# Four key groups moved into the first part's norms, six modulations on VectorE, token products of 512 columns

## Chip, cores and metric

One program runs on one core of a Trainium2 chip. The metric is the device time of one execution in microseconds; the runs before the change took 1834.9 to 1837.41 us, with a median of 1836.98.

## What is computed

Two transformer parts run one after the other on 256 tokens of width 1024, all in fp32. The reference, cut to what matters here:

```python
def first_block(x, c, ...):
    c_act = silu(c)                                    # one row of 1024
    for l in range(2):
        mod = c_act @ w_ada[l] + b_ada[l]              # six rows of 1024
        sh1, sc1, g1, sh2, sc2, g2 = split(mod, 6)
        h = rmsnorm(x, norm_mix_g[l]) * (1 + sc1) + sh1
        z = h @ w_in[l]
        o = concat([swa(z), mla(z), nsa(z), moba(z)])  # four attentions, 4 heads each
        x = x + g1 * (o @ w_out[l])
        h = rmsnorm(x, norm_mlp_g[l]) * (1 + sc2) + sh2
        x = x + g2 * (square(relu(h @ w_up[l])) @ w_down[l])
    return rmsnorm(x, final_norm_g)

def second_block(x, mem, ...):
    for l in range(2):
        z, xbc, dt, dq, dk, dv, dg, cq, cg, gl = split(x @ w_in[l])
        y_ssd, y_diff = ssd(z, xbc, dt), diff_attention(dq, dk, dv) * silu(dg)
        mk, mv = split(mem @ w_mem_kv[l])              # keys, values of 256 memory tokens
        y_cross = cross_attention(cq, mk, mv) * silu(cg)
        merged = sum of gates[i] * (branch i @ its weights)
        x = layernorm(ALPHA * x + merged @ w_out[l])
```

## The kernel before

**Weights.** Every weight passes once, as tiles `w` of 128 x 1024 fp32 (0.5 MB). The list `wq` holds them in the order in which they're used; `stream` appends to it. `next_w` takes the next one, and on the way loads the first 8 entries of the list (`AHEAD_W`, through SP's queue, into a ring of `NW` = 8 tiles) and splits the first 4: ScalarE rounds the tile to fp32r (`wh`, line 290), VectorE subtracts (`wl`, line 292). Products run as three fp32r matmuls, high by high, low by high and high by low. Tiles of the modulations (`w_ada`) and of the two compressions aren't split; they stay in their ring slot until they've been multiplied.

**Products.** `gemm` queues a product of 256 output columns as two pieces of 24 matmuls of 128x128 by 128x256, summed in one bank of PSUM. With `tok=True` tokens lie on the partitions: the activations are the loaded operand, 256 weight columns stream, and a bank holds both token halves. This form makes the memory's values, the difference attention's values `dv`, the last output, and two small products of the first part.

**The order of the work.** The queue `q` holds pieces under tags; `fill(n)` emits the next n, `need(tag)` all up to the last with that tag. The framework then orders each engine's instructions by priority (splits and norm chains stand higher) along a simulated timeline. What is left in `q` when a norm starts runs while the norm's chain (square, sum over partitions, power of -0.5, spread, scale, shift) goes through the other engines.

**Modulations.** Each of the twelve (layer, slot) pairs has four steps of two tiles. `ada_step` does them on TensorE (four blocks of 32 columns, fp32, two instructions each: 64 for a pair), `ada_pool` on GpSimd, as a product per partition and a sum, whose rows `ada_rows` adds up over the partitions with eight short matmuls; `ada_end` transposes the result into `mod`. GpSimd has (1,0), (1,1) and (1,5), during the feed-forward parts. TensorE has the other nine: (0,0) and (0,1) at the start, (0,2) to (0,4) in layer 0's attention, (0,5) in its second norm (tag `norm`), (1,2) and (1,3) between the layers (tag `next`), (1,4) in layer 1's second norm.

**The memory's keys and values.** `mem_gemm` makes them in eight groups of 256 columns, four of keys and four of values. Layer 0's six first groups run at the start, mixed with modulation steps, its last two in the first part's last norm, after the memory has been loaded again (`late_mem`). Layer 1's eight run at the end of layer 0 of the second part, whose layer norm asks for 2, 4 and 2 pieces between its steps and leaves the last eight to its scale and shift.

**Units.** Activations live in a ring of `NU` = 11 tiles of 128 x 2048 fp32. Three banks of PSUM (`gbank`) serve the products.

**The last output.** `finish` adds the residual and computes mean and variance by 256 columns, then normalizes.

## Time and profile before

| | |
|---|---|
| median of 3 runs | 1836.98 us |
| the profiled execution's own time | 1838.83 us |
| its span | 1837.0 us |
| mean granted clock of TensorE | 0.992 |
| instructions | 37186 |
| VectorE busy | 73% |
| ScalarE busy | 55% |
| GpSimd busy | 20% |
| read from HBM | 339.01 MB |

Times within the trace count from the span's start. Up to 61 us the start's products and modulations run, up to 205 layer 0's attention, up to 404 its feed-forward part; layer 1 goes from there to 746, and the second part from 770 to the end. Matmuls are pipelined, so a matmul's duration is longer than the step to the next. A wait for several semaphores is put down to the one that came last.

### The profile page before, as it was taken

To read this page: it belongs to the slowest core of one execution; us is meant where nothing else is said; L and a number is where in the kernel's file an instruction comes from. 1 tells how busy PE (TensorE), PEld (TensorE's weight loads), DVE (VectorE), ACT (ScalarE), POOL (GpSimd) and SP (SyncE) were. 2 spreads that over 40 slices of the span, in tenths; PEclk is the share of its full clock that TensorE was granted. 3 is DMA by queue.
4 is the path that set the end of the run, shared out by engine and by line. 5 is a ranking of instruction groups with operands and counts; after the bars stand their busy time and mean duration, and the time that the engine had idled before them with its cause. 6 is when DMAs were issued, how large, how long until landed. Compare 5 with 4: busy or idle time off the path is not lost.

```text
span 1837.0 us, 37186 instructions
## 1 busy us (share of the span) xinstructions
PE 1791.6 (98%) x14800; PEld 1696.7 (92%) x14800; DVE 1334.8 (73%) x2212; ACT 1017.1 (55%) x1882; POOL 358.9 (20%) x291
## 2 busy tenths in 40 slices
PE   7999999999998999999999999999999999999998
PEld 6878799987878999999999999999999999999998
DVE  4575775756778655798897897566687897997566
ACT  4354444444545444557777575454556687675552
POOL 0000271800007300002444202200001445202200
PEclk9999999999998999999999999999999999999999
DMA  9873886757447655554444644465553445554451
GB/s 335 317 246 129 301 272 197 258 197 294 130 138 282 230 182 183 168 171 140 143 162 154 191 161 148 166 205 175 193 175 130 148 160 162 181 166 168 153 183 60
DMA packets 98223, 346.88 MB, mean 189 GB/s; under 512 B 12288, under 2 KB 13440, under 8 KB 97792
## 3 DMA queue, kind: packets, MB, share of 16 engines
q1 hardware_dynamic: 98048, 344.50, 55.5%
q8 instruction: 116, 1.90, 0.4%
q14 instruction: 59, 0.48, 0.1%
HBM read 339.01 MB, written 1.05 MB: 185 GB/s over the span
## 4 chain that ended last, share of the span: by engine, by line
PE 90%; DVE 3%; ACT 2%; DMA 2%; issue 1%; POOL 0%; POOLq 0%; SPq 0%; DVEq 0%; ACTq 0%
PE g L318 68%; PE acc L318 10%; PE yps L318 2%; DVE wl L292 1%; PE sc L318 1%; PE ada L318 1%; PE ds L318 1%; PE o L318 1%; DMA w<-w_ada 1%; ACT wh L290 1%; PE do L318 1%; PE xs L318 1%; PE xo L318 1%; DMA w<-w_up 1%; PE tw L1153 1%
## 5 line engine op out<-in xcount | busy, mean ns | idle before, releaser
L292 DVE TENSOR_TENSOR wl<-w,wh 128x1024 fp32r<-128x1024 f32 x518 | 664.3, 1285 | 337.7 <-ACT wh L290 335.5
L290 ACT CAST wh<-w 128x1024 fp32r<-128x1024 f32 x518 | 540.6, 1047 | 510.9 <-PE g L318 328.3
L318 PE MATMUL g<-xh,wh 128*128 128x256 f32 x1664 | 477.1, 287 | 0.7 <-DVE cv L1234 0.4
L318 PE MATMUL g<-xl,wh 128*128 128x256 f32 x1664 | 472.3, 284 | 0.0
L318 PE MATMUL g<-xh,wl 128*128 128x256 f32 x1664 | 471.7, 284 | 0.0
L318 PEld LDWEIGHTS g<-xh,wh 128*128 128x128 f32 x1664 | 319.3, 192 | 13.0 <-issue 6.9
L318 PEld LDWEIGHTS g<-xl,wh 128*128 128x128 f32 x1664 | 319.4, 192 | 0.8 <-issue 0.7
L318 PEld LDWEIGHTS g<-xh,wl 128*128 128x128 f32 x1664 | 319.4, 192 | 0.1
L318 PE MATMUL g<-ah,wh 128*128 128x256 f32 x736 | 210.4, 288 | 4.2 <-ACT ah L552 4.2
L318 PE MATMUL g<-al,wh 128*128 128x256 f32 x736 | 210.6, 287 | 2.5 <-DVE al L553 2.5
L318 PE MATMUL g<-ah,wl 128*128 128x256 f32 x736 | 210.8, 287 | 0.7 <-DVE wl L292 0.7
L358 POOL TENSOR_TENSOR rsy<-rv,mhalf 128x2 f32<-128x2 f32 (+1 forms) x14 | 13.4, 958 | 938.8 <-DVE rv L375 831.1
L318 PE MATMUL acc<-pt,wh 128*128 128x256 f32 x1024 | 183.1, 280 | 0.0
L1452 POOL PARTITION_BROADCAST E<-rows x64 | 96.6, 1571 | 389.0 <-PE tw L1153 157.7
L1451 ACT ACTIVATE E<-E,ltok 128x128 f32<-128x128 f32 x384 | 124.5, 394 | 61.9 <-POOL E L1452 57.9
L318 PEld LDWEIGHTS acc<-pt,wh 128*128 128x128 f32 x1024 | 156.8, 188 | 0.4 <-issue 0.4
L318 PEld LDWEIGHTS g<-ah,wh 128*128 128x128 f32 x736 | 142.2, 194 | 8.0 <-ACT ah L552 4.4
L318 PEld LDWEIGHTS g<-al,wh 128*128 128x128 f32 x736 | 142.7, 194 | 4.5 <-DVE al L553 3.5
L318 PEld LDWEIGHTS g<-ah,wl 128*128 128x128 f32 x736 | 142.6, 194 | 1.3 <-DVE wl L292 1.1
L318 PE MATMUL acc<-pt,wl 128*128 128x256 f32 x512 | 142.3, 279 | 0.0
L531 POOL TENSOR_SCALAR sb<-w,ca 128x1024 f32<-128x1024 f32 x24 | 89.3, 3721 | 62.6 <-PE ada L318 32.8
L318 PEld LDWEIGHTS acc<-pt,wl 128*128 128x128 f32 x512 | 96.2, 188 | 0.0
(384 smaller groups left out, 3571.4 us busy)
## 6 DMA issues: line engine op xcount, KB each, us to landing
w<-w_ada SPq DMA_DIRECT2D x96, 512.0 KB
w<-w_up SPq DMA_DIRECT2D x64, 512.0 KB
w<-w_down SPq DMA_DIRECT2D x64, 512.0 KB
w<-w_br SPq DMA_DIRECT2D x64, 512.0 KB
w<-w_gl SPq DMA_DIRECT2D x48, 512.0 KB
w<-w_in SPq DMA_DIRECT2D x36, 512.0 KB
w<-w_mem SPq DMA_DIRECT2D x32, 512.0 KB
w<-w_out SPq DMA_DIRECT2D x32, 512.0 KB
```

The lines of the kernel that those rows point to most:

```text
L290: nc.scalar.copy(wh, w)
L292: nc.vector.tensor_tensor(wl, w, wh.bitcast(F32), ALU.subtract)
L318: self.nc.tensor.matmul(o, l, r, start=start, stop=stop)
L358: self.nc.gpsimd.tensor_tensor(y, v, self.mhalf[:, 0:cols], ALU.pow)
L531: nc.gpsimd.tensor_scalar(dst, w, ca[:, 2 * n + i : 2 * n + i + 1], None, ALU.mult)
L1153: nc.tensor.transpose(tps[:, kt * S + t * P : kt * S + (t + 1) * P], src[:, t, kt * P : (kt + 1) * P], e.ident)
L1451: ex = lambda o, s, r: nc.scalar.activation(o, o, AF.Exp, bias=bias[:, s, r : r + 1])
L1452: nc.gpsimd.partition_broadcast(E, state["rows"][32 * (h % 4) : 32 * (h % 4) + 1, :])
```

## The change

- **Keys.** The memory's weights are stored apart, keys in four groups of 256 columns (`w2_mk`), values in two of 512 (`w2_mv`). Layer 1's four key groups go into layer 0's second norm (group 0), into the step between the layers (1 and 2) and into layer 1's second norm (3). Their result has a unit of its own, `mk1`. The memory is loaded again in either layer's attention. At the end of layer 0 of the second part only the two value groups remain. At the start five of layer 0's groups run, the last of them 512 wide, and one remains for the last norm.
- **Modulations.** (0,5) and (1,0) to (1,3) go to VectorE in the first feed-forward part, (1,5) to VectorE in the second, by `ada_vec`: one multiply, then seven multiply-adds on 128x1024. `ada_rows` is queued when the eighth is emitted, so behind the pieces that are queued already. (1,4) goes into layer 1's attention, on TensorE.
- **Token products.** `tok_gemm` makes 512 columns: four pieces of two weight rows blocks for both token halves, each half in a bank of its own. It serves the memory's values, `dv` and the last output.
- **Rings.** `NW` falls to 6, `AHEAD_W` rises to 10, `NU` to 12.

```diff
-NW, NS = 8, 4
-AHEAD_W, AHEAD_S = 8, 4
+NW, NS = 6, 4
+AHEAD_S = 4
+AHEAD_W = NW + AHEAD_S
-NU = 11
+NU = 12
...
+    def _whole(self, ent):
+        return ent[0][0].startswith(("w_ada", "cmp_"))
...
-            if i < AHEAD_S and ent[3] is None:
+            if ent[3] is None and (i < AHEAD_S or self._whole(ent)):
                 self._split(ent)
...
+    def tok_mm(self, ps, t, act, k, w, j, st, sp):
+        wh, wl = (x[:, j * 512 : (j + 1) * 512] for x in w)
+        h, l = (x[:, k, t * P : (t + 1) * P] for x in act)
+        self.mm(ps, h, wh, st, False)
+        self.mm(ps, h, wl, False, False)
+        self.mm(ps, l, wh, False, sp)
+
+    def tok_gemm(self, tag, key, act, evac):
+        banks = []
+        def piece(n):
+            w = self.next_w(*key)
+            for t in range(2):
+                if n == 0:
+                    banks.append(self.gbank("g"))
+                for j in range(2):
+                    self.tok_mm(banks[t], t, act, 2 * n + j, w, j, n == 0 and j == 0, n == 3 and j == 1)
+                if n == 3:
+                    evac(banks[t], t)
+        for n in range(4):
+            self.add(tag, lambda n=n: piece(n))
...
+MEM_KEYS = lambda l: [("w2_mk", l, g) for g in range(4)] + [("w2_mv", l, g) for g in range(2)]
...
-    ad_early = lambda l: ada(l, 2) if l == 0 else []
+    ad_early = lambda l: ada(0, 2) if l == 0 else ada(1, 4)
...
-    MEM = 6
+    ad_mlp = lambda l: [k for p in ([(0, 5)] + [(1, s) for s in range(4)] if l == 0 else [(1, 5)]) for k in ada(*p)]
+    def mlp_keys(l):
+        out = {}
+        for j, key in enumerate(ad_mlp(l)):
+            out.setdefault(1 + (3 * j // 4 if l == 0 else 2 * j), []).append(key)
+        return out
+    MEM = 5
+    mem1 = MEM_KEYS(1)
+    filler = [mem1[0:1], mem1[3:4], mem1[1:3], MEM_KEYS(0)[MEM:]]
...
-        e.stream(("w_out1", l, 2), ("w_out1", l, 3), ("w_up", l, 0), *ad_norm(l))
+        e.stream(("w_out1", l, 2), ("w_out1", l, 3), ("w_up", l, 0), *filler[l], ("w_up", l, 1))
...
-    def ada_pool(l, s, n):
+    def ada_vec(l, s, n):
         if n == 0:
-            boxes[l, s] = e.t(ap_, [P, 1536], "sb", bufs=2)[:, 0:D]
+            i = boxes["n"] = boxes.get("n", -1) + 1
+            if i % 2 == 0:
+                boxes["rows"] = e.unit("rows")
+            boxes[l, s] = boxes["rows"][:, i % 2 * D : (i % 2 + 1) * D]
         rows = boxes[l, s]
         for i in range(2):
-            w = e.next_w("w_ada", l, s, n)
-            first = n == 0 and i == 0
-            dst = rows if first else e.t(ap_, [P, 1536], "sb", bufs=2)[:, 0:D]
-            nc.gpsimd.tensor_scalar(dst, w, ca[:, 2 * n + i : 2 * n + i + 1], None, ALU.mult)
-            if not first:
-                nc.gpsimd.tensor_tensor(rows, rows, dst, ALU.add)
+            w, c = e.next_w("w_ada", l, s, n), ca[:, 2 * n + i : 2 * n + i + 1]
+            if n == 0 and i == 0:
+                nc.vector.tensor_scalar(rows, w, c, None, ALU.mult)
+            else:
+                nc.vector.scalar_tensor_tensor(rows, w, c, rows, ALU.mult, ALU.add)
+        if n == 3:
+            e.add("mlp", lambda: ada_rows(l, s))
...
         e.need("I")
+        hl.append(load_mem(e))
         e.need("ad")
...
-        ada_add("norm", ad_norm(l))
+        mem_fill("norm", filler[l])
         bc0 = norm_stats(x)
         e.need("norm")
...
-        ada_add("next", ad_next(l))
+        mem_fill("next", filler[DEPTH + l])
...
-            e.gemm("dv", G("dv", g), act, ev_dv, tok=True)
+                nc.scalar.copy(dqk["dv"][:, t, g * 512 : (g + 1) * 512], ps)
+            e.tok_gemm("dv", ("w2_dv", l, g), act(0), ev_dv)
...
-        for g in range(8):
-            mem_gemm(e, l + 1, g, mhl, nmk, nmv)
+        for i in range(4, 6):
+            mem_gemm(e, l + 1, i, mhl, nmk, nmv)
```


## Rows read from the trace of the kernel before

**Rows 1.** The page: busy us (share of the span) and instructions of each engine.

```profile
PE 1791.6 (98%) x14800; PEld 1696.7 (92%) x14800; DVE 1334.8 (73%) x2212; ACT 1017.1 (55%) x1882; POOL 358.9 (20%) x291
```

**Rows 2.** Busy time by stage: stretch, its length, engines (instructions), TensorE's clock, DMA share, GB/s.

```profile
0.00:60.00 60.00, 49.24 (x430) 43.18 (x431) 25.34 (x38) 25.00 (x32) 1.81 (x5) 1.00 0.92 333
60.00:205.50 145.50, 141.64 (x1206) 117.41 (x1205) 94.85 (x281) 64.60 (x158) 1.40 (x2) 1.00 0.65 238
205.50:229.40 23.90, 20.31 (x176) 17.99 (x175) 18.50 (x29) 11.31 (x19) 13.44 (x6) 0.86 0.72 266
229.40:404.00 174.60, 174.38 (x1466) 172.46 (x1464) 114.57 (x102) 80.50 (x93) 83.31 (x26) 1.00 0.69 229
404.00:424.30 20.30, 17.49 (x195) 11.44 (x193) 11.13 (x26) 7.91 (x15) 0.72 (x1) 1.00 0.92 345
...
546.00:573.60 27.60, 19.74 (x176) 17.60 (x176) 19.80 (x31) 12.48 (x20) 12.81 (x6) 0.81 0.82 297
...
746.00:770.30 24.30, 22.24 (x173) 21.96 (x172) 17.31 (x37) 12.00 (x20) 0.72 (x1) 0.93 0.43 140
...
1270.50:1317.60 47.10, 47.10 (x397) 47.10 (x396) 32.83 (x46) 25.84 (x35) 0.73 (x1) 1.00 0.55 180
```

**Rows 3.** Timeline of modulations: start, us, engine, line, tiles, count [idle, releaser].

```profile
205.63 3.66 PE L318 MATMUL ada<-w,ca 128*32 128x256 f32 x64
...
408.78 0.64 PE L318 MATMUL ada<-w,ca 128*32 128x256 f32 x8 [1.07 <-DMA w<-w_ada]
```

**Rows 4.** The table by stretches again, at either clock level.

```profile
216.00:220.00 4.00, 4.00 (x21) 4.00 (x20) 3.63 (x7) 1.81 (x4) 3.61 (x2) 0.50 1.02 415
1250.00:1260.00 10.00, 10.00 (x85) 10.00 (x85) 6.48 (x8) 3.99 (x4) 0.00 (x0) 1.00 0.48 155
```

**Rows 5.** Timeline of TensorE, plain fp32 scores of the cross attention.

```profile
805.30 2.54 PE L318 MATMUL xs<-mk,cq 128*128 128x256 f32 x11
```

**Rows 6.** Groups by shape: two of the token products' forms, count | busy, mean ns.

```profile
L318 PE MATMUL g<-wh,xh 128*128 128x256 f32 x128 | 37.3, 292 | 0.0
...
L318 PE MATMUL g<-wh,gh 128*128 128x256 f32 x64 | 17.9, 283 | 0.0
```

**Rows 7.** Timeline of layer 1's second norm, 552 to 560 us.

```profile
552.26 1.23 DVE L292 TENSOR_TENSOR wl<-w,wh 128x1024 fp32r<-128x1024 f32 x1 [3.03 <-ACT wh L290]
...
554.39 1.22 PE L318 MATMUL bc<-pack,rsy 128*128 128x128 f32 x4 [4.04 <-POOL rsy L358]
...
557.88 0.17 DVE L958 SCALAR_TENSOR_TENSOR A<-mod,pack 128x8 f32<-128x8 f32 x1
...
559.15 0.80 PE L318 MATMUL g<-ah,wh 128*128 128x256 f32 x2 [2.90 <-ACT ah L552]
```

**Rows 8.** Timeline of the start and of the first norm's end.

```profile
52.16 1.93 PE L318 MATMUL ada<-w,ca 128*32 128x256 f32 x30
...
60.31 0.40 PE L318 MATMUL g<-ah,wh 128*128 128x256 f32 x2
...
213.79 0.38 PE L318 MATMUL g<-ah,wh 128*128 128x256 f32 x1 [1.31 <-ACT ah L552]
```

**Rows 9.** Groups by shape, 235 to 400 us, VectorE and GpSimd.

```profile
L292 DVE TENSOR_TENSOR wl<-w,wh 128x1024 fp32r<-128x1024 f32 x58 | 83.6, 1446 | 54.9 <-ACT wh L290 54.9
...
L531 POOL TENSOR_SCALAR sb<-w,ca 128x1024 f32<-128x1024 f32 x13 | 49.6, 3813 | 47.9 <-PE ada L318 32.8 <-DMA w<-w_ada 14.1
```

**Rows 10.** The same of VectorE, 1180 to 1320 us.

```profile
L292 DVE TENSOR_TENSOR wl<-w,wh 128x1024 fp32r<-128x1024 f32 x49 | 59.9, 1224 | 31.2 <-ACT wh L290 30.9
```

**Rows 11.** Instructions on tile r: count, ns min/median/max, first and last start, form.

```profile
L1182 DVE SCALAR_TENSOR_TENSOR r<-r,mv,gb x2: 1274/1275/1276, 1826.0 to 1831.0; 128x1024 f32<-128x1024 f32 x2
```

**Rows 12.** Waits of SP's queue: us in total, times, longest.

```profile
SPq L280 <- PE ada L318: 82.3, 39, 15.5
```

**Rows 13.** Timeline of the first part's last norm.

```profile
742.44 0.87 DVE L1029 SCALAR_TENSOR_TENSOR x<-acc,mod,x 128x256 f32<-128x256 f32 x2
...
760.57 0.58 PE L318 MATMUL dt<-xh,wh 128*128 128x256 f32 x1 [1.01 <-ACT xh L419]
```

More of the change, by code (lines that the diff above doesn't have):

```diff
@@ L270, in stream @@
         for key in keys:
-            self.wq.extend([key, i, None, None] for i in range(1 if key[0] == "w2_dt" else 2))
+            self.wq.extend([key, i, None, None] for i in range(self.d[key[0]].shape[-1] // 1024))
     def _fetch(self, ent):
@@ L541, in ada_add @@
         for key in keys:
[L542 removed]
+            e.add(tag, lambda key=key: (ada_vec if tag == "mlp" else ada_step)(*key[1:]))
     def norm_stats(src):
@@ L667, in out, with mem_fill @@
                     e.split(oh[:, base + c, :], ol[:, base + c, :], o[c][:, :S])
+    hl = []
+    def mem_fill(tag, steps):
+        for key in steps:
+            mem_gemm(e, key[1], MEM_KEYS(key[1]).index(key), hl[-1], *((mk0, mv0) if key[1] == 0 else (mk1, None)), tag)
     def mixers(l, ah, al, oh, ol, ev_x):
@@ L1004, in down_last @@
                     part(c, (m, m + 1))
-        def late_mem():
-            with tc.issue_after(last["dve"].ins), tc.issue_after(last["act"].ins):
-                box.append(load_mem(e))
-        parts, box, last = {}, [], {}
+        parts = {}
         steps = mlp_keys(l)
         for g in range(17):
-            if l + 1 == DEPTH and g == 1:
-                e.add("mlp", late_mem)
             if g < 16:
@@ L1119, in block2 @@
             e.stream(a, b)
-        for a, b in zip(W("xs"), W("dv")):
-            e.stream(a, b)
+        for g, a in enumerate(W("xs")[0:4]):
+            e.stream(a, *W("dv")[g // 2 : g // 2 + g % 2])
         for g, a in enumerate(W("cg")):
@@ L1131, in block2 @@
             e.stream(("w2_gl", l, 4 + g), ("w2_br1", l, g))
-        e.stream(*W("out"))
+        e.stream(*(W("out") if l + 1 < DEPTH else [("w2_last", 0, g) for g in range(2)]))
         if l + 1 < DEPTH:
-            e.stream(*[("w2_mem", l + 1, g) for g in range(8)])
+            e.stream(*MEM_KEYS(l + 1)[4:])
     def soft(scs, scale):
```

98 lines of the change are left out of this document (44 added, 54 removed).

## The prediction, made before the changed kernel ran

> **What bounds the kernel now.** I read the engine table first: TensorE is busy 98% of the span, in 14,800 matmuls, so time goes only where matmuls leave the stream or where holes in it close [rows 1]. The table by stages comes next, because the holes aren't spread evenly [rows 2]. The second part of the model (770 us to the end) has none to speak of: in 1270.5 to 1317.6 TensorE works 47.10 of 47.10 us. The holes lie in the first part: the first norm (205.5 to 229.4) works 20.31 of 23.9 us at a mean granted clock of 0.86, layer 1's norm before its feed-forward part (546 to 573.6) 19.74 of 27.6 at 0.81, the step from layer 0 to layer 1 (404 to 424.3) 17.49 of 20.3. The third reading is DMA: 0.92 busy in the first 60 us and 0.92 in 404 to 424.3, both of which load modulations, against 0.55 around 1290 [rows 2].
>
> **Unit prices.** A split product takes 128x256 matmuls. In 10 us at granted clock 1.00 the table counts 85, with one overlapping at either end: (10 + 0.28) / 85 = 0.12 us from one to the next [rows 4]. One group of 256 columns is 48 of them, 5.76 us; one piece (half a group) 2.88 us. A modulation on TensorE is 64 short matmuls, 3.66 us [rows 3]; the eight that add up its finished rows are 0.64 us with their drain [rows 3].
>
> **Wide products.** At a granted clock of 0.50 (1.2 GHz) 21 matmuls of 256 columns fill 4 us plus an overlap of 0.4: 0.21 us each, which is 256 columns at 1.2 GHz and nothing more [rows 4]. At 2.4 GHz the columns would take 0.107, but 0.12 is measured; so at full clock something beside the columns, per matmul, is the limit, and where the columns take 0.21 it hides. A matmul with 512 columns at full clock takes 0.213 in columns. The plain fp32 matmuls of the cross attention support this: two passes over 256 columns per loaded weight, 11 in 2.54 us, (2.54 - 0.38) / 10 = 0.216 [rows 5]. So I take 0.216 against 2 x 0.12 = 0.24: 0.024 saved per wide matmul. The bounds: 0.24 (no saving) and 0.12 (columns cost nothing more; the rival below). The forms `g<-wh,xh` (128) and `g<-wh,gh` (64) each stand three times (high and low parts), the former's pattern again for the memory's rows: 384 + 384 + 192 = 960 narrow matmuls become 480 wide [rows 6]. 96 wide ones make one place: 2.3 us.
>
> The Trainium skill, page "TensorE: Matmul & The Clock Gate", section "Back-to-back issue gap", gives a sustained 131 ns per matmul at 512 columns in a stream of weight loads and matmuls, and 216 ns for one isolated. By the first, the 480 would save 480 x (240 - 131) = 52 us, an estimate from that page; no row here shows it, and the half-clock row speaks for the second.
>
> **Part by part.**
>
> (1) Start, 0 to 61. Same work, but five key groups instead of six stand there, the last with four pieces, and the last two modulation steps come behind it. Now the last steps run at 52.16, and a sixth group of 5.76 us hides the way to the first `ah` matmul at 60.31 [rows 8]. Afterwards the steps end some 5 us later (two more pieces before them) and nothing hides the copy, transposes, scale and shift. From the end of the steps to the first `ah` matmul it's 60.31 - 54.09 = 6.2 us, in part a place in TensorE's queue behind the group; I charge 5 of them, so the dense stretch starts 4 to 5 us later than at 61. The raw ring shrinks from 8 to 6 tiles while DMA is 0.92 busy, and SP already waits 39 times, 82.3 us in all, for modulation tiles to be read [rows 12]. I take +5; bounds 0 and +10.
>
> (2) Layer 0's mixers. Modulations (0,2) to (0,4) keep their places, with a ring of 6: the eight tiles of (0,4) no longer fit ahead. Two tiles come late by about a transfer; plus 1 MB of memory loaded once more through SP's queue, with its two casts and two subtractions (1.2 us each [rows 10]) on ScalarE and VectorE; the weights behind it in SP's queue have landed well ahead by the table (0.65 busy [rows 2]). +2; 0 to +5.
>
> (3) First norm. 3.66 us of modulation [rows 3] give way to a key group of 5.76; the chain to the first matmul at 213.79 [rows 8] stays, so the extra 2.1 us fall into its hole. The dense filler should leave less of the half clock (0.86 mean). -2; -4 to 0.
>
> (4) First feed-forward part and the step to layer 1. Five modulations are 40 VectorE operations of 128x1024. The nearest row is the same operation on 128x1024 in the last norm, 1.275 us [rows 11]: 51 us. VectorE is busy 114.6 of 174.6 us there [rows 2], with its `wl` at 1.446 us [rows 9] against 1.224 where GpSimd is quiet [rows 10]; with GpSimd's 3.8 us multiplications gone [rows 9], 62 x 0.22 = 14 us come back. 114.6 + 51 - 14 = 152 of 174.6: hidden. DMA goes from 0.69 to about 0.85. A new wait stands in VectorE's queue: an operation whose tile is late holds the next `wl` and TensorE behind it, as in [rows 7]; weights are split four tiles (11.5 us) ahead, so I charge nothing for it and leave up to 5 us in the bound. Adding up the rows is queued behind the last product, five x 0.64 = 3.2 us, 1.3 of it there before, and the residual update waits for (0,5). Two key groups (11.5 us) instead of two modulations (about 8) then cover the norm; the hole of 1.07 for DMA [rows 3] and others, 2.8 in all, close. Net +2.5; 0 to +8.
>
> (5) Layer 1's mixers take (1,4) in: 3.66 + 0.64 for its end, and 0.7 of wait for its tiles, in DMA's 1.07 of [rows 3] the nearest row. +5; +3 to +8.
>
> (6) Layer 1's norm before its feed-forward part. Here 4.04 us go on a chain that is visible: VectorE's queue holds `wl` of the next weights (which waited 3.03 for its tile) ahead of the norm's variance, so `bc` starts at 554.39; then A waits for the modulation (1,4) until 557.88 and the first matmul comes at 559.15 [rows 7]. With (1,4) done in the mixers and no modulation tiles before the weights in DMA, both go; 5.76 us of keys stand in for 3.66. What is late next is the norm's chain itself, as in the first norm, 3.6 us shorter: 27.6 - 23.9 = 3.7 [rows 2], and 2.3 from the filler and clock. -6; -9 to 0, if the memory's reload is late.
>
> (7) Last norm of the first part. The update starts at 742.44 under the last product [rows 13]; added up behind it, (1,5) delays it to the product's end (746) and by some 1.5 us for its own way, 5 in all; of the values left to do, 4 x 2.59 us, I let 3.5 hide it. +1.5; -1 to +3.
>
> (8) End of the second part's layer 0. The filler falls from 16 pieces to 8: -8 x 2.88 = -23.0. The eight left are wide: 2.59 each, -2.3. The pieces between the norm's steps are those eight, so they still cover its two sums. Only the scale and shift lose their cover. Its price is that of the last norm of the first part, which has no cover there either: 24.3 us for 165 matmuls x 0.12 plus 0.8, so 3.7 lost, a short stretch at half clock included (0.93) [rows 2]; the first product starts at 760.57 and follows the chunks [rows 13]. With two slower operations per chunk I take +4.5. Sum -20.8; with 0 or 9 for the uncovered part, -25 to -16.
>
> (9) Other wide products: values of the difference attention in both layers and the last output, 3 x -2.3; the last evacuation is 512 wide and follows whole, +0.5. -6.4; 0 to -7.
>
> **Sum.** 5 + 2 - 2 + 2.5 + 5 - 6 + 1.5 - 20.8 - 6.4 = -19.2. The profiled execution takes 1838.83 us (span 1837.0 and 1.8 around it), which is 1.9 above the median of 1836.98; it becomes 1819.6, on the median's scale 1818.
>
> **Rivals.**
> - *Wide matmuls cost 0.24.* For it: no row here has split matmuls of 512 columns; against it, the half-clock row and the plain fp32 one. The terms (8) and (9) lose 9: 1827. Chance 0.10.
> - *Late keys.* Reloaded memory or its tiles arrive after the holes, in (3) and (6): the 8 us there aren't won: 1826. Against it: they're loaded in the mixers. Chance 0.08.
> - *The raw ring of 6, the slower side.* Modulation tiles hold their slots until they're multiplied, so a run of more than 6 tiles stops the loads behind it. If every six such tiles cost a turnaround of 3.5 us (landing plus split), the start's 16 with their neighbours pay 4 x 3.5, the mixers' 24 in layer 0 another 4, layer 1's 8 one or two: 9 to 10 turns, 33 us, of which my terms (1), (2) and (5) hold 10: 1818 + 23 = 1841. It decides from 19 us beyond my terms. For it: the 82.3 us of SP's waits [rows 12]; against it: other loads and matmuls run meanwhile. Chance 0.12 for slower by this.
> - *VectorE becomes the bound in (4).* TensorE needs 96 x 0.12 = 11.5 us per step of the feed-forward part, VectorE 101 / 15.1 = 6.7 and 2.67 operations: bound from 1.8 us each. At twice the row's 1.275 us it would be 13.5, + 15 x 2.0: 1848. Chance 0.05.
> - *512 columns for the time of 256:* 480 x 0.12 = 57.6 instead of 11.5, 1772. By its rule the page named above stands for nearly this. Chance 0.02.
>
> **Numbers.** My forecast has 0.63, with its own range 1805 to 1831. Below 0.2% (3.7 us) a measurement of this kernel can't tell a change. Faster: 0.62 from the forecast, 0.08 and 0.07 from the first two rivals, 0.02 from the last: 0.79. Same 0.07, slower 0.14. The range for 8 in 10: 1802 to 1838.
>
> **What would show it.** Steps of `g<-xh,wh` with 512 columns at 0.216; no `ada` group in the three norms; `bc` within 2.5 us of `st` in the layer-1 norm; a stretch of about 26 us in place of 47.1 at the end of layer 0, followed by a short hole; VectorE at 0.85 in the first feed-forward part with TensorE at 1.0; the first `ah` matmul near 65. I'm wrong if TensorE shows new holes of over 20 us in the first 205 us, or if it waits for `wl` in 229 to 404.

## The result, and the profile after

The changed kernel takes 1864.47 us (median of 4 runs, 1859.18 to 1866.53) against 1837.20 (4 runs, 1834.90 to 1838.98): ratio 1.0137, 95% interval [1.0118, 1.0155]. It is slower by 27 us; the forecast was 1818, faster. The profiled execution spans 1863.7 us, 26.7 more than the 1837.0 of before, and is split up here by landmarks of TensorE's stream (first and last matmul of each part):

"Forecast" is what the prediction's terms give for a stretch; two entries cover several stretches, as they say.

| stretch | before | after | change | forecast |
|---|---|---|---|---|
| start, to the first `ah` product | 60.3 | 63.5 | +3.2 | +5 |
| layer 0's mixers | 145.1 | 149.1 | +4.0 | +2 |
| first norm, to the first feed-forward product | 8.4 | 11.6 | +3.2 | -2 |
| layer 0's feed-forward, to the last down product | 190.1 | 205.1 | +15.0 | +2.5, with the next line |
| step to layer 1's first product | 10.3 | 20.1 | +9.8 | |
| layer 1's mixers | 131.8 | 136.5 | +4.7 | +5 |
| layer 1's norm and feed-forward | 200.0 | 199.1 | -0.9 | -6 |
| last norm of part one, to `dt` | 14.7 | 21.8 | +7.1 | +1.5 |
| part two, layer 0, to its last output product | 509.9 | 509.4 | -0.5 | -6.4, with "part two, layer 1" and "after the last matmul" |
| end of that layer | 47.9 | 26.4 | -21.5 | -20.8 |
| part two, layer 1, to the last matmul | 511.0 | 510.4 | -0.6 | |
| after the last matmul | 7.6 | 10.8 | +3.2 | |

The gain at the end of part two's layer 0 came as forecast. Twice that was lost elsewhere, above all in and behind layer 0's feed-forward.

The page's engine line (answers to [rows 1]): 648 matmuls fewer, of which 480 come of pairs put into one and the rest of modulations that left TensorE. Its busy time is only 3.2 us less, while the span grew by 26.7.

```profile
PE 1788.4 (96%) x14152; PEld 1675.9 (90%) x14152; DVE 1348.0 (72%) x2254; ACT 1018.7 (55%) x1884; POOL 211.8 (11%) x246
```

The table by stages, in the columns of [rows 2] and for the same stages: stretch, length, engines with their instructions, TensorE's clock, DMA share, GB/s.

```profile
0.00:63.50 63.50, 48.49 (x384) 40.52 (x384) 25.64 (x38) 25.46 (x33) 1.85 (x5) 1.00 0.84 306
63.50:212.70 149.20, 143.14 (x1202) 120.61 (x1203) 97.22 (x283) 67.24 (x160) 1.40 (x2) 0.97 0.66 235
212.70:245.80 33.10, 25.71 (x181) 23.93 (x180) 26.75 (x40) 14.79 (x23) 1.65 (x1) 0.90 0.61 200
245.80:429.30 183.50, 172.69 (x1418) 169.78 (x1416) 124.79 (x122) 76.92 (x87) 0.00 (x0) 0.99 0.79 268
429.30:459.40 30.10, 27.77 (x233) 25.72 (x232) 21.66 (x42) 15.22 (x26) 0.70 (x1) 0.94 0.49 159
586.00:613.40 27.40, 21.53 (x156) 20.61 (x155) 20.55 (x35) 12.66 (x20) 0.70 (x1) 0.88 0.48 156
785.00:814.30 29.30, 22.15 (x114) 18.99 (x113) 19.64 (x43) 12.55 (x22) 0.70 (x1) 0.83 0.37 116
1316.20:1342.00 25.80, 24.10 (x115) 19.98 (x113) 18.64 (x25) 13.79 (x17) 0.72 (x1) 1.00 0.54 184
```

The fourth line is the one to look at. TensorE worked 174.38 of 174.6 us there; now 172.69 of 183.5, with 48 matmuls fewer (24 of the first products moved ahead of this window, and 24 for the sums of two modulations stand behind it). VectorE is busy 124.79 us, 0.68 of it: it isn't short of time, but TensorE waits for it. The next view says why: the waits of VectorE and then of TensorE between the first feed-forward product and the last down product (us in total, times, longest).

```profile
DVE rows L585 <- DMA w<-w_ada: 39.7, 18, 4.5
DVE rows L583 <- DMA w<-w_ada: 14.3, 4, 4.4
...
PE acc L332 <- DVE pt L1032: 6.7, 3, 2.4
PE g L332 <- DVE wl L306: 4.7, 8, 1.0
```

VectorE stands 54.0 us in front of modulation tiles that have not landed, and behind these instructions stand the splits `wl` and the squared activations `pt` that TensorE needs. TensorE's waits in that stretch are 15.3 us in all, against 2.5 in the kernel before. The timeline (start, us, engine, line, [idle, releaser]) shows first four lines of VectorE from the norm ahead, where the same instructions stand between those of the scale and shift; then one place where VectorE waits, and TensorE's wait that follows from it:

```profile
226.04 1.28 DVE L585 SCALAR_TENSOR_TENSOR rows<-w,ca,rows 128x1024 f32<-128x1024 f32 x1
227.24 0.48 DVE L605 SCALAR_TENSOR_TENSOR nt<-x,A,bc 128x256 f32<-128x256 f32 x1
227.63 0.48 DVE L607 SCALAR_TENSOR_TENSOR al<-nt,mod,ah 128x256 fp32r<-128x256 f32 x1
228.03 1.28 DVE L585 SCALAR_TENSOR_TENSOR rows<-w,ca,rows 128x1024 f32<-128x1024 f32 x1
...
299.40 1.22 DVE L306 TENSOR_TENSOR wl<-w,wh 128x1024 fp32r<-128x1024 f32 x1
304.19 0.75 DVE L583 TENSOR_SCALAR rows<-w,ca 128x1024 f32<-128x1024 f32 x1 [3.57 <-DMA w<-w_ada]
304.86 1.22 DVE L306 TENSOR_TENSOR wl<-w,wh 128x1024 fp32r<-128x1024 f32 x1
...
311.07 1.28 DVE L585 SCALAR_TENSOR_TENSOR rows<-w,ca,rows 128x1024 f32<-128x1024 f32 x1 [0.87 <-DMA w<-w_ada]
...
313.41 0.68 DVE L1032 TENSOR_TENSOR pt<-pt,pt 128x512 fp32r<-128x512 f32 x1
...
314.15 0.38 PE L332 MATMUL acc<-pt,wh 128*128 128x256 f32 x1 [2.11 <-DVE pt L1032]
```

The step to layer 1 is told by its timeline. The row sums start when the last down product is out (429.50); the residual update, which overlapped the last products before, starts at 432.34; the transposes of the sums (`adat`) are strewn among the pieces of the key groups, and the squares (L446) wait for them because both use the two buffers of one tile. The sum `st` comes 16.5 us after the sums' start.

```profile
429.50 1.50 PE L332 MATMUL ada<-rows,ones 128*32 128x256 f32 x22
432.34 3.23 DVE L1081 SCALAR_TENSOR_TENSOR x<-acc,mod,x 128x256 f32<-128x256 f32 x8
437.68 0.50 PE L332 MATMUL adat<-pack,pt 128*128 128x4 f32 x4
438.27 0.64 ACT L446 ACTIVATE pt<-x 128x512 f32<-128x512 f32 x1 [0.65 <-PE adat L332]
...
446.00 0.51 PE L332 MATMUL st<-ones,fold 128*128 128x1 f32 x4
449.43 0.50 PE L332 MATMUL g<-ah,wh 128*128 128x256 f32 x2 [1.11 <-ACT ah L606]
```

The wide products, in the last output: a stretch with its matmul count, and then the group by shape (count | busy, mean ns).

```profile
1831.60:1852.60 21.00, 21.00 (x94) 17.38 (x93) 11.30 (x14) 5.76 (x6) 0.00 (x0) 1.00 0.00 1
```
```profile
L332 PE MATMUL g<-wh,gh 128*128 128x512 f32 x32 | 12.3, 389 | 0.0
```

94 in 21.0 us, with an overlap of 0.39: (21.0 + 0.39) / 94 = 0.2275 us each. Two narrow ones took 2 x 0.12 [rows 4], so 0.0125 is saved, half of the 0.024 in the forecast. The tail lost 3.2 us: the last column statistics (0.69 us, twice the columns) now stand in VectorE's queue behind the first half's 1.27 us normalisation:

```profile
1854.04 1.27 DVE L1232 SCALAR_TENSOR_TENSOR r<-r,mv,gb 128x1024 f32<-128x1024 f32 x1
1855.23 0.69 DVE L1224 BATCH_NORM_STATS2 stats<-r 128x6 f32<-128x512 f32 x1
```

### The profile page after: what moved, and what is told of

Read it like the earlier page. It is cut to its first block, busy times and chain, and to the rows that moved or that the text cites. A ratio compares the mean times of both kernels' runs of the same rounds, so it can differ in the third digit from the quotient of the medians.

```text
span 1863.7 us, 35889 instructions
## 1 busy us (share of the span) xinstructions
PE 1788.4 (96%) x14152; PEld 1675.9 (90%) x14152; DVE 1348.0 (72%) x2254; ACT 1018.7 (55%) x1884; POOL 211.8 (11%) x246
## 4 chain that ended last, share of the span: by engine, by line
PE 77%; DVE 9%; DMA 8%; ACT 3%; issue 3%; POOL 0%; POOLq 0%; SPq 0%; DVEq 0%; ACTq 0%
PE g L332 59%; PE acc L332 6%; DMA w<-w_ada 5%; DVE wl L306 4%; ACT wh L304 1%; PE yps L332 1%; PE ds L332 1%; PE o L332 1%; DMA w<-w_out 1%; PE do L332 1%; PE ada L332 1%; DMA w<-w_in 1%; PE xo L332 1%; PE sc L332 1%; PE xs L332 1%
## 5 line engine op out<-in xcount | busy, mean ns | idle before, releaser
L306 DVE TENSOR_TENSOR wl<-w,wh 128x1024 fp32r<-128x1024 f32 x518 | 639.9, 1239 | 295.1 <-ACT wh L304 293.2
L332 PEld LDWEIGHTS g<-ah,wh 128*128 128x128 f32 x736 | 143.8, 197 | 10.9 <-ACT ah L606 6.6
L1277 DVE SCALAR_TENSOR_TENSOR cv<-g,pack,cv 128x254 f32<-128x254 f32 (+1 forms) x192 | 88.8, 476 | 2.2 <-ACT cv L1274 0.7
```

The costliest lines, as they stand in the source:

```text
L306: nc.vector.tensor_tensor(wl, w, wh.bitcast(F32), ALU.subtract)
L332: self.nc.tensor.matmul(o, l, r, start=start, stop=stop)
L1277: nc.vector.scalar_tensor_tensor(a_[:, a:b], p_[:, a + j - 2 : b + j - 2], conv_w[:, i0 + j : i0 + j + 1], a_[:, a:b], ALU.mult, ALU.add)
```

## The experiments

All medians stand beside runs of the kernel before on the same chip (1838.5, 1839.2, 1840.2, 1840.3, 1840.0 and 1840.1 in the six groups); "FF" is layer 0's feed-forward by the landmarks above, "step" the one to layer 1, "mix 1" layer 1's mixers, "norm L" the last norm of part one. Stage times are of one profiled execution each. Layer 0's mixers show how far such a time strays: the same code, with six places in the ring, took 145 to 151 us in these kernels. The feed-forward strays less (189.4 to 190.1 in three kernels that leave it alone). The expectations of no_ada_wait, no_ada_vec and ring7 go by the stretches of the stage table instead (33.1 us for the norm with the first products, 183.5 for the rest of the feed-forward).

| kernel | median us | ratio to before, 95% | FF | step | mix 1 | norm L |
|---|---|---|---|---|---|---|
| before | 1837.2 | | 190.1 | 10.3 | 131.8 | 14.7 |
| after | 1864.5 | 1.0137 [1.0118, 1.0155] | 205.1 | 20.1 | 136.5 | 21.8 |
| rows_in_place | 1857.0 | 1.0100 [1.0085, 1.0115] | 205.9 | 14.6 | 140.1 | 14.0 |
| no_ada_wait | 1894.1 | 1.0314 [1.0291, 1.0337] | 231.9 | 20.1 | 136.1 | 21.8 |
| no_ada_vec | 1844.7 | 1.0038 [1.0023, 1.0053] | 194.2 | 20.1 | 136.3 | 21.8 |
| ring7 | 1880.1 | 1.0227 [1.0212, 1.0242] | 202.6 | 20.1 | 139.8 | 22.1 |
| wl_first | 1852.4 | 1.0072 [1.0051, 1.0094] | 199.2 | 16.2 | 143.7 | 14.0 |
| wl_first_resident | 1843.0 | 1.0027 [1.0012, 1.0042] | 194.7 | 14.7 | 144.0 | 14.0 |
| keys_at_end | 1860.0 | 1.0100 [1.0070, 1.0130] | 206.3 | 11.3 | 137.8 | 14.0 |
| before_wide | 1841.0 | 1.0006 [0.9990, 1.0023] | 189.4 | 11.2 | 133.1 | 14.7 |
| combo | 1848.7 | 1.0048 [1.0029, 1.0068] | 202.6 | 16.3 | 138.4 | 14.0 |
| before_one_key | 1848.0 | 1.0048 [1.0031, 1.0064] | 189.7 | 11.0 | 131.8 | 14.7 |
| before_pool_key | 1898.8 | 1.0320 [1.0298, 1.0343] | 237.8 | 18.5 | 131.1 | 14.7 |
| cols_apart | 1842.9 | 1.0017 [1.0002, 1.0032] | 200.7 | 14.8 | 136.2 | 14.0 |
| six_vec | 1855.8 | 1.0086 [1.0070, 1.0102] | 215.7 | 16.3 | 130.7 | 14.0 |
| four_vec | 1833.1 | 0.9970 [0.9950, 0.9989] | 190.1 | 14.7 | 137.4 | 14.0 |
| pool_two | 1839.4 | 0.9994 [0.9979, 1.0010] | 194.9 | 16.0 | 136.2 | 14.0 |
| cols_apart_ring7 | 1855.7 | 1.0084 [1.0055, 1.0113] | 191.8 | 16.3 | 139.0 | 14.0 |

**rows_in_place: the row sums where they are ready.**

```diff
-            e.add("mlp", lambda: ada_rows(l, s))
+            e.q.insert(min(6, len(e.q)), ("mlp", lambda: ada_rows(l, s)))
```

> Only the place of the row sums changes: the TensorE step that turns a finished modulation row into columns is queued six pieces behind the last VectorE step instead of at the end of the queue. Theory B (the row sum behind the last down product holds the residual update): the step from the last down product of layer 0 to layer 1's first product falls from 20.1 to 11 to 13 us, the last norm of part one from 21.8 to 15 to 17 us, nothing else moves, in all 13 to 16 us, about 1850 us. Rival (the update is late because VectorE's own queue waits for weight tiles): under 3 us of these, 1861 us or more.

The step fell by 5.5 and the last norm by 7.8 us: 13.3, near the least that theory B allows, with more of it in the norm and less in the step than expected. The total fell by 7.5 only, where 13 to 16 were expected: layer 1's mixers took 3.6 more, and the feed-forward stayed. So the place of the row sums is shown as a cause of 13 us in these two stages; what the mixers gave back isn't explained.

**no_ada_wait and no_ada_vec: VectorE's instructions without their tiles, and the tiles without the instructions.**

```diff
-            w, c = e.next_w("w_ada", l, s, n), ca[...]
+            e.next_w("w_ada", l, s, n)
+            w, c = flat(x[:, 0:4, :]), ca[...]
...
-            else:                                     # no_ada_vec alone
-                nc.vector.scalar_tensor_tensor(rows, w, c, rows, ALU.mult, ALU.add)
```

> Leaves out the real modulation values: VectorE's modulation instructions stay, 48 of the same shape in the same places, but read the resident residual stream instead of the fetched tiles; the tiles are still fetched. So their VectorE time stays and their waits for transfers go, and each raw tile is free when it lands. Theory A (VectorE's in-order queue stands behind a late tile, and the weight splits with it): the feed-forward of layer 0 falls from 183.5 to 174 to 177 us, the norm ahead of it from 33.2 to 29 to 31 us, in all 9 to 13 us, about 1853 us. Rival 1 (VectorE's time itself is the bound): within 3 us of 1864.5. Rival 2 (the transfers are the bound): also within 3 us.

> Leaves out 42 of the 48 modulation instructions on VectorE (the first of each modulation stays, on a resident tile), keeps all the fetches. Theory A: within 3 us of the kernel with the resident operand in the feed-forward, and 4 to 6 us less in the norm ahead of it, where some six of them stand between the scale-and-shift instructions: about 1847 us. Rival 1 (VectorE's time): most of the 18.9 us that the feed-forward and the step behind it lost come back only here, 1845 us, with the kernel with the resident operand still at 1862 or more. Rival 2 (the transfers): both stay at 1862 or more.

The first missed by 40 us, and not for a rival's reason. With nothing to wait for, the instructions were ordered as early as possible: all 40 start between 220 and 271 us, beside the norm's scale and shift and the first products of a feed-forward that lasts from 219 to 451. In this stretch, from the norm on, VectorE is busy 61.96 of 65 us, TensorE 32.66.

```profile
206.00:271.00 65.00, 32.66 (x177) 29.65 (x175) 61.96 (x73) 15.86 (x24) 1.65 (x1) 0.66 0.33 107
```

So it says nothing on waits, but much on order: the same instructions, crowded into the stage's start, cost 27 us more in the feed-forward. The second kept the transfers and gave 10.9 us of the feed-forward's 15 back; the 4.1 that are left stand beside the transfers. By the letter the two results together are rival 1's, but the first kernel changed VectorE's order, so they don't decide between waits and VectorE's time. wl_first and wl_first_resident do.

The norm ahead is as long without the modulation instructions (11.6), so its +3.2 isn't theirs. `st`, the sum over partitions, starts 6.6 us after the mixers' last product instead of 3.8. Two things hold it. The filler's matmuls, 5.64 us where the modulation took 3.28, stand ahead of it in TensorE's queue. And VectorE's sum of squares is done 6.4 us after that product instead of 3.1, so that `st` waits 0.55 us more. Two weight splits stand in VectorE's queue among the squares, where the kernel before has none: the filler uses split weights, and as its products end they let ScalarE's next cast go, and the split behind it. The modulation's tiles weren't split. The end of the sum and `st` in the kernel before, then the same of after with the splits ahead:

```profile
208.10 0.43 DVE L399 TENSOR_TENSOR fold<-fold 128x256 f32<-128x256 f32 x1
...
209.22 0.60 PE L318 MATMUL st<-ones,fold 128*128 128x1 f32 x4
```
```profile
214.37 1.22 DVE L306 TENSOR_TENSOR wl<-w,wh 128x1024 fp32r<-128x1024 f32 x1
215.74 1.05 ACT L304 CAST wh<-w 128x1024 fp32r<-128x1024 f32 x1 [0.55 <-PE g L332]
216.82 1.23 DVE L306 TENSOR_TENSOR wl<-w,wh 128x1024 fp32r<-128x1024 f32 x1 [0.63 <-ACT wh L304]
...
218.68 0.42 DVE L439 TENSOR_TENSOR fold<-fold 128x256 f32<-128x256 f32 x1
219.25 0.58 PE L332 MATMUL st<-ones,fold 128*128 128x1 f32 x4 [0.55 <-DVE fold L439]
```

**ring7: one more raw buffer in the change's own order.**

```diff
-NW, NS = 6, 4
+NW, NS = 7, 4
...
+        nrm = e.t(ap_, [P, 1536], "sb", bufs=2)     # cqn and ckn in it; pct in tile nt; part two: E bufs 3, lt bufs 1
```

> One raw weight buffer more, seven instead of six, by moving three small tiles of part one into existing buffers and taking one softmax buffer and one small buffer from part two (so part two may lose some us and is not compared). Theory C (the ring of six makes the fetches late, and so VectorE waits): VectorE's waits for modulation tiles in the feed-forward of layer 0 fall from 52 us to under 30, and that stage from 183.5 to 176 to 180 us. Rival (VectorE's order is planned too early, whatever the ring): the stage stays within 2 us of 183.5.

The edit takes `AHEAD_W` from 10 to 11 as well. The result is nearer the rival: 2.5 us off the feed-forward, VectorE's waits for tiles 47.0 instead of 54.0, where under 30 were expected. Layer 0's mixers fell from 149.1 to 143.2; as that stage strays, the ring may count there, but it isn't shown. Part two, with two small buffers less, took 10.7 us longer in each layer.

**wl_first and wl_first_resident: VectorE's order, with and without the tiles.** Both on top of rows_in_place.

```diff
+            with tc.issue_after(e.last_wl.ins):      # the latest weight split written; same engine
                 if n == 0 and i == 0:
                     nc.vector.tensor_scalar(rows, w, c, None, ALU.mult)
...
+            w, c = flat(x[:, 0:4, :]), ca[...]       # wl_first_resident alone
```

> The kernel with the row sums in place, and each modulation instruction on VectorE is ordered behind the latest weight split already written (the same engine, so no new wait between engines). That takes them out of the scale-and-shift of the first norm and puts one behind each one or two splits in the feed-forward. Theory A2 (their place in VectorE's order is what costs): from the first product of layer 0's feed-forward to its last down product 205.9 falls to 193 to 197 us, total 1845 to 1849 us from 1857. Rival 1 (late transfers, which the order does not change): that stage stays at 202 or more, VectorE still waits over 35 us for modulation tiles. Rival 2 (VectorE's time): also 202 or more, without such waits.

> As the kernel with the splits first, but the modulation instructions read the resident residual stream (the modulation values are left out); VectorE's order stays the same and the tiles are still fetched. Theory A2: within 2 us of the kernel with the splits first in that stage. Rival 1 (late transfers): 5 us or more below it. Rival 2 (VectorE's time): 202 or more in both.

With the order alone the feed-forward fell by 6.7 us, less than the 9 to 13 I expected and more than the rivals allow; VectorE no longer waits for modulation tiles at all. Without the tiles another 4.5 go, close to rival 1's 5. (The profiled execution of that kernel was 8 us above its median, so no other stage of it is read.) So both count, the order and the tiles that land late. VectorE's time is not the bound at this order: with all 40 instructions and no wait the stage takes 194.7 us, with 5 of them (no_ada_vec) 194.2. What is left of TensorE's waits in wl_first is new:

```profile
PE adat L332 <- ACT pt L565: 2.6, 3, 1.7
PE ada L332 <- DVE rows L586: 2.6, 1, 2.6
```

The gain was partly given back in layer 1's mixers, 143.7 us with a clock of 0.93 (before: 131.8 at 0.99). There the mixers' own weights come late, as I read it behind the early (1,4) tiles in the ring (combo moves these tiles, and has no such wait), and TensorE stands for 2.92 us; the next 13.7 us run at half clock (timeline, then that stretch in the columns of the stage table):

```profile
459.38 1.04 ACT L304 CAST wh<-w 128x1024 fp32r<-128x1024 f32 x1 [2.55 <-DMA w<-w_in]
460.47 0.58 PE L332 MATMUL g<-wh,ah 128*128 128x256 f32 x1 [2.92 <-ACT wh L304]
```
```profile
460.50:474.20 13.70, 13.70 (x34) 7.13 (x35) 3.48 (x4) 2.21 (x3) 0.00 (x0) 0.51 0.40 135
```

**keys_at_end: what a filler in the step is worth.**

```diff
-    filler = [mem1[0:1], mem1[3:4], mem1[1:3], MEM_KEYS(0)[MEM:]]
+    filler = [mem1[0:1], mem1[3:4], [], MEM_KEYS(0)[MEM:]]
-        for i in range(4, 6):
+        for i in (1, 2, 4, 5):
```

> The kernel with the row sums in place, and the two key groups of the step to layer 1 go back to the end of the second part's layer 0. If a filler group is hidden wholly, the step keeps its 14.6 us and the end of layer 0 grows by 11.5: 1868 us. Worked out from before, where the step took 10.3 us with 6.0 of it idle: the step falls to 9.5 to 10.5, the end grows from 26.4 to 37 to 38, 1864 us, so two groups of 11.5 us are worth 7. Rival (a filler in a norm gains nothing): 1857 us, within 2.

The step fell by 3.3, to 11.3; the end grew by 8.9, to 35.3 (11.5 of matmuls less the holes of 2.3 that they close). By stages two groups in the step are worth 5.6 us, where 7 were expected. The totals differ by 3, which these intervals don't resolve.

**before_wide: term (9) by itself.** The three wide products put into the kernel before, as in the change's diff.

> The kernel before with the wide token products alone (values of the difference attention, layer 1's memory values, last output): 480 narrow pairs become 480 wide ones. By the step of 0.227 us read in the changed kernel's last output, 480 x 0.013 = 6.4 us less, and 2 to 3 us more behind the last product, since the last evacuation is one of 512 columns: 1834 us from 1838. By the forecast's 0.216 it would be 11.5 less, 1829. Rival (the tail eats it): within 1 us of before.

No change: the rival. The end of layer 0 fell by 1.2 us, layer 1 by 1.0, layer 0's value product gained nothing, and the tail took 2.9 more (10.5 after the last matmul).

**combo: three small causes, one stage each.** On wl_first.

```diff
-            e.q.insert(min(6, len(e.q)), ...)
+            e.q.insert(min(12, len(e.q)), ...)
-    ad_early = lambda l: ada(0, 2) if l == 0 else ada(1, 4)
+    ad_early = lambda l: ada(0, 2) if l == 0 else []      # and (1,4) into ad_mix; last output in 256 columns
```

> The kernel with the splits first, and three more edits, each read in its own stage: the row sums stand 12 pieces behind the last VectorE step instead of 6; modulation (1,4) stands in the later half of layer 1's mixers instead of the early half; the last output takes 256 columns again. Theory: TensorE's waits for row sums (2.6 + 2.6 us) were the six pieces, so the feed-forward of layer 0 falls from 199.2 to 194 to 196; the early (1,4) tiles stood in a ring of six ahead of the mixers' own weights (a wait of 2.55 us for w_in, then 13.7 us of half clock), so layer 1's mixers fall from 143.7 to 134 to 138; the tail behind the last product goes back from 10.8 to 7.6 and the product costs 1.3 more. In all about 1840 us. Rival for the mixers (the clock falls whatever the loads): 142 or more.

The mixers (138.4 from 143.7, just above the range) and the tail (7.9) did as expected. The feed-forward didn't: it rose to 202.6, and the total is 9 us above the expected. TensorE's queue now stands 6.8 us at the transposes of the sums, and 10.2 us at the lower clock level, in two stretches, follow two of these waits:

```profile
PE adat L331 <- ACT pt L564: 6.8, 4, 3.2
```

**before_one_key and before_pool_key: the change's idea, from the other side.** The kernel before with one key group moved into layer 1's norm; and with (1,4) on GpSimd as well.

```diff
+            mk1 = v3(e.unit("mk"), KC)                    # both
+            mem_gemm(e, 1, 0, box[0], mk1, None, "norm")
-    ad_mlp = lambda l: [(1,0),(1,1)] if l == 0 else [(1,5)]       # before_pool_key
+    ad_mlp = lambda l: [(1,0),(1,1),(1,4)] if l == 0 else [(1,5)]
-    mlp_keys = lambda l: {1 + 6 * i + n: ...}
+    mlp_keys = lambda l: {1 + 4 * i + n: ...}                   # the sums stay at g == 6 * i + 8
```

> The kernel before with one key group of layer 1's memory moved from the end of the second part's layer 0 into the norm ahead of layer 1's feed-forward, behind modulation (1,4), and nothing else. That norm took 13.2 us, 6.3 of it idle and 6.9 at half clock; the group is 5.76. If it falls into the hole: the norm stays within 2 us, the end falls by 5.8, 1834 us from 1839. Rival (the chain of that norm waits for the group): no change.

> As the kernel before with one key group moved, and modulation (1,4) goes from that norm to GpSimd in layer 0's feed-forward, as its third there; its sum of rows stands behind the step to layer 1. GpSimd is busy 83 us for two of the three there, so some 125 of 190. Expected: that norm 10 to 12 us instead of 13.2, the end of layer 0 less 5.8, layer 0's feed-forward within 2 us: 1830 us. Rival (GpSimd's work slows VectorE's splits, or its raw tiles starve the weights): the feed-forward grows by 3 us or more and eats it.

In the first the norm grew by 2.0 and the end fell by 5.7, as hoped; but part two's layer 0 took 520.6 instead of 509.9. The keys occupy a unit of the general ring that part two had for itself. I take that to be the cause: the changed kernel holds its keys in the same way but has twelve units, and its part two took 509.4. It wasn't tried by itself. In the second the feed-forward grew by 47.7 us, the rival's side, but by a flaw of this kernel. GpSimd adds up in one of two buffers, and I moved its modulations closer together while the first two row sums, which free the buffer, stayed where they were. So GpSimd waits 96.8 us for TensorE's sums, and TensorE waits for the casts of weights, which I read as late because GpSimd's raw tiles hold their places meanwhile (the group of GpSimd's multiplications with the idle time before them, then TensorE's waits between 215 and 440 us):

```profile
L531 POOL TENSOR_SCALAR sb<-w,ca 128x1024 f32<-128x1024 f32 x23 | 79.7, 3467 | 105.7 <-PE ada L318 96.8 <-DMA w<-w_ada 7.0
```
```profile
PE g L318 <- ACT wh L290: 17.0, 8, 4.5
PE g L318 <- DVE wl L292: 6.6, 11, 1.4
```

It shows what a blocked modulation can cost, even with a ring of eight, and nothing of a third modulation's own price.

**cols_apart, six_vec, four_vec, pool_two, cols_apart_ring7: how much the feed-forward can take.** All on combo, with the transposes apart from the sums:

```diff
     def ada_rows(l, s):
         blocks(ps, ones32, boxes[l, s], True, True)
-        ada_end(l, s, ps)
+        nc.scalar.copy(row, ps[:, 0:S])
+        e.q.insert(min(3, len(e.q)), ("mlp", lambda: ada_cols(l, s, row)))
```

- cols_apart has the change's 40 instructions on VectorE in this stage.
- six_vec has 48: (1,4) comes from TensorE.
- four_vec has 32: (1,3) goes to TensorE, in layer 1's mixers.
- pool_two has 24, with (1,2) and (1,3) as 30 instructions on GpSimd. (It and four_vec hold the summed row in another small tile.)
- cols_apart_ring7 has 40 and `NW` = 7, paid for as in ring7.

> The kernel with the three further edits, and the four small transposes that follow ScalarE's copy of a summed modulation row stand three pieces behind the sum instead of right behind it in TensorE's queue. Theory: the 7.3 us that TensorE waits there for the copy go, and half of the 14.3 us of half clock with them: the feed-forward of layer 0 falls from 202.6 to 192 to 196 us, total 1839 to 1842 from 1848.7. Rival (the transfers are late, the wait only moves): 200 or more.

> As the kernel with the transposes apart, and modulation (1,4) goes from TensorE in layer 1's mixers to VectorE in layer 0's feed-forward: 48 instead of 40 instructions there. If VectorE's time is not the bound: the feed-forward within 3 us of the kernel with five, the mixers 4 us less, total 1836 to 1838. Rival (VectorE's time or the transfers are near their limit there): the feed-forward grows by 6 us or more, total no better.

> As the kernel with the transposes apart, but modulation (1,3) is done by TensorE in layer 1's mixers: 32 instead of 40 modulation instructions on VectorE in layer 0's feed-forward. If VectorE with its transfers is at its limit there: that stage falls from 200.7 to 192 to 195 us; layer 1's mixers grow by some 4.3; total 1838 to 1840. Rival (a fixed cost of the order): the stage stays within 2 us of 200.7 and the total grows by 3 to 5.

> As the kernel with the transposes apart, but two of the five modulations of layer 0's feed-forward, (1,2) and (1,3), are done by GpSimd (as two were before the change), so VectorE has 24 instead of 40 instructions there, at the same transfers. If VectorE's time is the limit: the stage falls to 192 or less, total near 1834. Rival (the ring of six: a tile waits 3.8 us on GpSimd and holds its place, and the weights come late): the stage grows by 3 us or more, as with three modulations on GpSimd, where it took 237.8.

> The kernel with the transposes apart and 40 modulation instructions on VectorE, with a raw ring of seven instead of six (bought as before, so part two loses some 20 us and is not compared). If the ring is the limit: at 6.67 tiles per step of 11.5 us a place may take 12.1 us with seven, 10.4 with six, and 11.3 was enough with 32 instructions; so layer 0's feed-forward falls from 200.7 to 189 to 193 us and TensorE's waits there from 10 to under 3. Rival (VectorE's own time or the rate of the transfers): 198 or more.

The feed-forward's stretch in four of them, in the columns of the stage table (cols_apart, six_vec, four_vec, cols_apart_ring7):

```profile
220.10:420.80 200.70, 193.15 (x1591) 188.81 (x1592) 146.11 (x160) 86.91 (x110) 0.00 (x0) 0.98 0.79 268
```
```profile
223.00:438.70 215.70, 200.57 (x1604) 194.19 (x1605) 155.35 (x169) 87.44 (x110) 0.00 (x0) 0.96 0.78 269
```
```profile
222.70:412.80 190.10, 189.62 (x1574) 187.22 (x1574) 138.45 (x151) 87.87 (x107) 0.00 (x0) 0.99 0.78 261
```
```profile
218.80:410.60 191.80, 190.62 (x1592) 187.46 (x1593) 146.02 (x160) 88.57 (x109) 0.00 (x0) 0.99 0.81 280
```

In cols_apart the waits at the transposes went, but the stage fell by 2 us only; others took their place (3.5 for `pt`, 2.7 for `rows`): the rival. With 32 instructions the stage is as short as before the change, and with 48 it is 15 us longer than with 40. The last line speaks for the ring: VectorE has the same 146 us of work as in the first, the same tiles come in, at 280 instead of 268 GB/s, and one place more takes the stage from 200.7 to 191.8. So neither VectorE's time nor the rate of the transfers held cols_apart, but how soon six places come free. (The edit also takes `AHEAD_W` from 10 to 11; that wasn't tried by itself.)

An estimate from these stages says the same. The stage fetches 64 weight tiles and one tile per modulation instruction. With 40 and with 48 instructions it takes the same time per tile, 200.7 / 104 and 215.7 / 112, both 1.93 us, so one of six places is used again every 11.6 us. To keep to the 190.1 us of before, a place may take 6 x 190.1 / 104 = 11.0 us with 40 and 10.2 with 48, which is too little, but 11.9 with 32 and, with seven places, 12.8 with 40, which is enough. (The expectation of cols_apart_ring7 has 11.3 for 32 instructions; it spreads their tiles over 15 steps, the edit over 14, and by that count it is 11.0, against 10.4 for 40.)

pool_two was to relieve VectorE and didn't: it has 16 modulation instructions fewer there, but beside GpSimd's work its splits take 1541 ns instead of 1222 (mean; pool_two and cols_apart), and it is busy 157.4 of 195 us, more than in cols_apart. The stage fell to 194.9, between the two forecasts, all the same. That is one more sign against VectorE's time as the bound; what a place's 11.6 us consist of isn't settled.

four_vec beats both kernels: 0.9970 [0.9950, 0.9989] of the kernel before, 7 us.

## Why the prediction was wrong

**The step that failed is (4)**, layer 0's feed-forward and the step to layer 1: +2.5 forecast, +24.8 measured: 22.3 of the 45.9 us between forecast and result.

- *"weights are split four tiles (11.5 us) ahead, so I charge nothing for it and leave up to 5 us in the bound."* The wait was seen and priced at 0, at most 5. Taking it out by order alone gave 6.7 us (wl_first), taking the late tiles out too another 4.5; all instructions with their waits are 10.9 by no_ada_vec. The splits are written four tiles ahead, but VectorE's queue is in order, and 22 of the modulation instructions found their tile missing, for up to 4.5 us, with one or two splits and the squared activations right behind. I counted VectorE's time (152 of 174.6 forecast, 124.8 of 183.5 measured: there was room) and not the order in which it is spent.
- *The ring of six* was a rival, for the start and the mixers, where its price of 23 us beyond my terms did not appear: (1), (2) and (5) were forecast +12 and measured +11.9 (3.2, 4.0 and 4.7 for 5, 2 and 5, so the sum is closer than its parts). I didn't ask it of the feed-forward, where the change takes the tiles fetched from 80 to 104 in 16 steps while the places go from 8 to 6. cols_apart_ring7 shows it there, at 8.9 us, once the order is mended; in the change's own order ring7 gained 2.5.
- *"Adding up the rows is queued behind the last product ... the residual update waits for (0,5)."* Right as a mechanism, and mis-sized: I took it as covered by the two key groups. The update starts 3.1 us after the last product, and then the squares stand behind transposes that stand behind pieces of those groups; 5.5 us came back with rows_in_place. And the two groups, 11.5 us, lengthen the step by 3.3 and shorten the end by 8.9 (keys_at_end), so they are worth 5.6. Besides, the 24 matmuls for the sums of two modulations, which stood among the feed-forward's products before, now stand in the step.

The other terms:

- (3) and (6), -8 forecast, +2.3 measured. (3) took the norm's chain as given. The filler, 5.64 us, is longer than the chain to `st`, 3.1 us in the kernel before, and it lengthens that chain to 6.4 by the splits that it lets in; that the filler's length and these splits make up the 3.2 us is read from the trace and wasn't tried. In layer 1's norm the waits of [rows 7] did go, but modulation instructions of (1,5) took their place: they stand in VectorE's queue ahead of the squares' sum, and TensorE waits 3.3 us for it (`st` at 595.83); without them (no_ada_vec) this norm is 4.1 us shorter. "Late keys" was the rival with nearly the right sum (0 for both) and the wrong reason: TensorE's waits in these norms are for `st`, `bc` and `ah`, and only 0.2 us for a key tile's split.
- (7) +1.5, measured +7.1: the same row sum; with it in place the last norm took 14.0, less than before.
- (8) -20.8, measured -21.5. Right in its mechanism, shorter filler and an uncovered scale and shift; the sum is closer than its parts. The wide pieces saved 1.1 us less than forecast (96 x 0.2275 = 21.8 for 20.7), and the uncovered part left holes of 2.3 where 4.5 were charged.
- (9) -6.4, measured +2.1 (before_wide, alone: nothing). 0.216 per wide matmul was 0.2275. The prediction let what a matmul costs beside its columns hide behind 512 of them; by its own 0.107 and 0.213 for the columns it is there in both forms, some 0.014 of either 0.12 or 0.2275, and joining a pair saves it once. The Trainium skill's 131 ns ("TensorE: Matmul & The Clock Gate", section "Back-to-back issue gap") does not hold for this stream of split matmuls; its isolated 216 ns is nearer, and 11.5 ns short. And I charged 0.5 us for the last evacuation, which cost 2.9 to 3.2.
- The clock, which I had only as a gain in the norms: the mean is 0.985 against 0.992. In the mixers of layer 0 it went from 1.00 to 0.97 and of layer 1 from 0.99 to 0.96. Holes of 2.7, 2.0 and 2.3 us that end at 132, 520 and 568 us are each followed within 1.5 us by 3.4 us at the lower level, as was one of 2.1 in the kernel before (ending at 483); but two of such length there (2.05 ending at 88, 2.4 at 530) were not. So what decides it stays open, as does how much of the two mixers' +8.7 is the clock.

Of my two signs of being wrong, the waits for `wl` in the feed-forward came: 4.7 us, and 6.7 for `pt`. VectorE was to be 0.85 busy there with TensorE at 1.0; it was 0.68, with TensorE at 0.94.

## What to carry to other kernels

Before moving work to an engine with spare time, write down what stands behind each moved instruction in its in-order queue, and when its operand lands there: spare time says nothing on a wait at the head of a queue. Prefetch buffers are a rate: places times the stage's time, divided by the tiles it fetches, is the time one place may take from one tile to the next, and here, by the estimate above, 11.9 us was enough and 11.0 was not. A filler is worth the hole, not its own length: measure the hole's chain (here 3.1 us to the sum of squares), and ask what the filler itself sets going in the queues of that chain.

## What the runs showed of the hardware that was not expected

- Split matmuls of 512 columns with a weight load each: 0.2275 us from one to the next at full clock, 0.0125 less than two of 256.
- After a hole of 2.92 us in layer 1's mixers (wl_first) 13.7 us ran at the lower level, though TensorE was never idle in them: the 16 matmuls of `uq` took 8.1 us there, 4.4 in the kernel before.
- The same split on VectorE, 128x1024, took 1222 ns in cols_apart, 1446 in the kernel before and 1541 in pool_two, where GpSimd multiplied and added beside it.
- Two small buffers less in part two (a fourth one of the softmax, a second one of the last norm) and a raw place more went with 10.7 us more in each of its layers (ring7; 8.3 and 12.1 from cols_apart to cols_apart_ring7).
